# Attention-times-values of the odd mixer: unsplit fp32 products of 64 columns in place of split products of 128

## The chip, the cores and the metric

The kernel runs on one NeuronCore of a Trainium2 chip. The metric is device time in microseconds of one execution; lower is better. The engines are named as the profile names them: PE (TensorE, the matrix array), PEld (its weight loads), DVE (VectorE), ACT (ScalarE), POOL (GpSimd), SP (SyncE, which issues most DMAs).

## The reference, cut to what matters

The program is a two-layer encoder trunk over 512 tokens of width 1024, all in fp32. Each layer runs a half-step FFN, a token mixer, attention into 256 memory tokens, and a second half-step FFN, each followed by a layer norm. The mixer of the odd layer (`mixer_c`) is the part concerned: 16 heads of width 64, where each token attends to a clamped window of 8 rows by 16 columns of the 8 x 64 token grid, with a learned bias.

```
q, k, v = split(h @ w_in, 3)                     # 512 x 1024 each, 16 heads x 64
for each grid row r, column c and head:
    s = q . k_nb * 64**-0.5 + bias               # 8 x 16 = 128 neighbours
    p = softmax(s)
    o = p @ v_nb                                 # the products that change
y = o @ w_out
```

## The kernel before, in words

**Numbers.** Operands of most products are split in two: a part `hi`, which is the value rounded to the reduced format fp32r (ACT writes it: a `CAST`), and the rest `lo` (DVE subtracts). The usual product is then three products of the array: hi·hi, hi·lo, lo·hi (`mm3`). Tokens are ordered by grid column, so that a tile of 128 tokens is 16 grid columns of 8 rows.

**The odd mixer.** Heads go in eight pairs. For each pair `queries` and `keys` project and split; `weights_of` makes the scores in PSUM tiles `a` for four blocks of 128 queries and at most 256 keys, adds the bias, and does the softmax on DVE, ACT and POOL; `turned` transposes the probabilities of both heads on PE into PSUM tiles `t` (two banks a head, 16 transposes a pair) and takes them out into SBUF; `attend` multiplies them with the values into PSUM tiles `d`; the results, split, are the stationary operands of the output projection (`share` for the first four pairs, `down` for the rest). `values(grp, t)` makes the values of four heads for one tile of 128 tokens; there are four groups and four tiles.

In `attend` there are for each head four tiles `j` of 128 keys, and each meets 256 queries. The values are kept split with the two parts side by side: 64 columns of hi and 64 of lo for each head, so one stationary operand has 128 columns. The probabilities are split too, so each (head, j) takes two products of 128 columns by 256, sixteen for a pair. The two halves of a result (partitions 0 to 63 from the hi values, 64 to 127 from the lo values) are then added: ACT copies one half, DVE adds the other, and the sum is split again.

**What sets the order.** The kernel records all its instructions as a graph and a planner (`Graph.plan`) writes out an order for each engine: it keeps a clock for every engine, adds a cost for each instruction (`Graph.cost`), and takes the ready instruction with the smallest key (the place in the program, or in the second pass a latest start worked back from PE's order). Tiles come from rotating pools: 27 SBUF buffers `slab` of 4 KB a partition, 14 buffers `t2` of 2 KB, PSUM banks `a` 3, `d` 2, `t` 3; who needs a buffer waits until an earlier user is done. All instructions are issued from one line, 157 (160 after the change), so groups in the profile are told apart by their tiles: `d<-slab,slab 128x256` in the odd mixer are the products of `attend`, `t<-ident,t` the transposes of `turned`, `t<-xh,slab`, `d<-xh,slab` and the like the projections, `slab<-t` what takes a PSUM bank out (the name `t` stands for a PSUM bank and for the `t2` buffers).

Of the kernel before, what the change touches and what calls it, by code (L numbers as in the profile page):

```python
# [12 lines left out]
F32 = mybir.dt.float32  # L13
F32R = mybir.dt.float32r
# [3 lines left out]
ALU = mybir.AluOpType  # L18
AX = mybir.AxisListType

P = 128
# [44 lines left out]
class Graph:  # L66
# [3 lines left out]

    LATENCY = {"tensor": 200.0, "vector": 115.0, "scalar": 135.0, "gpsimd": 90.0, "sync": 90.0}
    PATIENT = ("vector", "scalar")
    URGENT = ("vector", "scalar", "gpsimd")
    ENGINES = ("tensor", "vector", "scalar", "gpsimd", "sync")

# [36 lines left out]
    @staticmethod  # L112
    def cost(engine, method, out, ins, kw):
        n = 1
        for d in (out if method != "tensor_reduce" else ins[0]).ap[1:]:
            n *= d[1]
        wide = any(z.space == bass.MemoryType.PSUM for z in ins + [out]) if engine != "sync" else False
        if method == "dma_start":
            return 1200.0 if "accum_op" in kw else 600.0
        if engine == "tensor":  # L120
            return max(n / 2.4 + 14, 111)
        scalars = sum(1 for z in ins if z.ap[-1][1] == 1)
        aside = 120.0 * any(Graph.extent(z)[0] > 0 for z in ins + [out])
        if engine == "vector":
            if method == "tensor_scalar" and not wide:
                n = n / 2
            return n / 0.96 + 72 + aside + 60 * scalars + 120 * (method == "scalar_tensor_tensor" and "accum_out" in kw)
        if engine == "scalar":
            scaled = 42 * hasattr(kw.get("scale"), "tensor")
            return n / 1.2 + (55 if wide else 100) + aside + 45 * scalars + 130 * ("accum_out" in kw) + scaled  # L130
        if n <= 8:
            return 270.0 if method == "tensor_scalar" else 200.0 if method != "tensor_tensor" else 390.0 + 157.0 * n
        if method == "memset":
            return n * 0.83 + 60
        dense = len(ins) == 2 and all(z.ap[-1][0] != 0 for z in ins)
        return n * (2.4 if dense else 1.7) + (70 if dense else 130)

    def record(self, engine, method, args, kw):
        kw = dict(kw)
        aps = [z for z in list(args) + list(kw.values()) if hasattr(z, "tensor")]  # L140
        outs = [kw[k] for k in ("out", "accum_out") if k in kw]
        if "out" not in kw:
            outs.insert(0, args[0])
        ins = [z for z in aps if not any(z is o for o in outs)]
        op = Op()
        op.engine, op.index, op.dma, op.adds = engine, len(self.ops), method == "dma_start", "accum_op" in kw
        op.rank = op.index
        op.ns = self.cost(engine, method, outs[0], ins, kw)
        func = args[2] if method == "activation" else None
        op.table = str(func) if func in (AF.Silu, AF.Exp) else None  # L150
        op.size = math.prod(outs[0].shape) * 4
        op.thin = op.dma and engine == "sync" and op.size >= 2**19 and outs[0].shape[0] <= 64
        op.port = method in ("tensor_tensor", "scalar_tensor_tensor", "tensor_scalar") and (
            engine == "gpsimd" or engine == "vector" and math.prod(outs[0].shape[1:]) >= 64 and all(z.space != bass.MemoryType.PSUM for z in ins)
        )
        fn = getattr(getattr(self.nc, engine), method)
        op.call = lambda: fn(*args, **kw)  # L157
        op.deps, op.users, op.frees, op.later = set(), [], [], []
        if self.after and engine in self.after[1]:
            op.deps.add(self.after[0])  # L160
        for z, writes in [(z, False) for z in ins] + [(z, True) for z in outs]:
            info = self.tiles.get(z.tensor.name)
            if info is None:
                continue
            p0, p1, runs = self.extent(z)
            opens = writes and kw.get("start", False)
            keep = []
            for q, w, a0, a1, other in info["log"]:
                over = opens or p0 < a1 and a0 < p1 and (
                    info["bank"] and q.engine != engine or any(l < b and a < h for l, h in runs for a, b in other)  # L170
                )
                if over and (w or writes or info["bank"] and q.engine != engine) and q is not op:
                    op.deps.add(q)
                covered = writes and p0 <= a0 and a1 <= p1 and all(any(l <= a and b <= h for l, h in runs) for a, b in other)
                if not covered:
                    keep.append((q, w, a0, a1, other))
            keep.append((op, writes, p0, p1, runs))
            info["log"] = keep
            info["users"].add(op)
        self.ops.append(op)  # L180

    def plan(self):

# [38 lines left out]
        while len(order) < len(self.ops):  # L222
            best = None
            for e in self.ENGINES:
                arrive(e)
                if ready[e] and e in self.PATIENT:
                    key, _, op = ready[e][0]
# [72 lines left out]
    def emit(self):  # L300
# [10 lines left out]
        for op in self.ops:  # L311
            if op.engine in self.URGENT:
                op.key = last[op]
# [7 lines left out]
class Kernel:  # L321
# [925 lines left out]
    def mixer_c(self, ln_i, last):  # L1247
        nc, a = self.nc, self.a
# [4 lines left out]
        def values(grp, t):  # L1253

            if t == 0:
                wv[0] = self.w_cols_side(w_in, 2 * D + 256 * grp)
                vp[grp] = [self.slab(F32R, (P, 2, 4, 2, 64)) for _ in range(2)]
                if grp == 0:
                    for dst, lo in ((slice(64, 128), 0), (slice(0, 64), 448)):
                        nc.scalar.copy(ends[0][:, :, dst], self.xh[:, :, lo : lo + 64])  # L1260
                        nc.vector.tensor_copy(ends[1][:, :, dst], self.xl[:, :, lo : lo + 64])
            ps = self.ps("t" if grp else "a")
            for k in range(KB):
                x = self.xT(k, 64 + t * P, 64 + (t + 1) * P) if t < 3 else [z[:, k, :] for z in ends]
                self.side_step(ps, x, wv[0][k // 2][:, k % 2], k)
            z, y = vp[grp][t // 2][:, t % 2], self.t2(F32)
            self.side_sum(y[:, :256], ps)
            self.split(y[:, :256].rearrange("p (v c) -> p v c", v=4), z[:, :, 0], z[:, :, 1])

        def queries(pair, first=False):  # L1270

# [81 lines left out]
        def turned(us):  # L1353

            pts = []
            for u in us:
                part = lambda t, j: u[t][:, j * P : (j + 1) * P]
                banks = [
                    [part(0, 1), part(1, 0), part(1, 1), part(2, 0)],
                    [part(2, 1), part(3, 0), part(0, 0), part(3, 1)],  # L1360
                ]
                got = [self.split_t2(self.transposed([(i * P, P, z) for i, z in enumerate(bank)])) for bank in banks]
                pts.append(got)
            return pts

        def attend(pts, pair):
            pos = [self.ps("d") for _ in range(2)]
            for s, po in enumerate(pos):
                for j in range(4):
                    dst = po[:, j * P : j * P + 256] if j < 3 else po.rearrange("p (c n) -> p c n", c=4)[:, 0:4:3]  # L1370
                    v = vp[pair // 2][j // 2][:, j % 2, 2 * (pair % 2) + s].rearrange("p z c -> p (z c)")
                    for i, z in enumerate(pts[s][j // 2]):
                        mv = z[:, (j % 2) * 256 : (j % 2) * 256 + 256]
                        mv = mv.rearrange("p (c n) -> p c n", c=2) if j == 3 else mv
                        nc.tensor.matmul(
                            dst, v, mv, start=j == 0 and i == 0, stop=j == 3 and i == 1, skip_group_check=True
                        )

            o = self.t2(F32)
            for s, po in enumerate(pos):  # L1380
                y = o[64 * s : 64 * s + 64]
                nc.scalar.copy(y, po[64:128])
                nc.vector.tensor_tensor(out=y, in0=po[0:64], in1=y, op=ALU.add)
            return self.split_pair(o)

        def share(n):

# [5 lines left out]
        vp, qs, ks, acts = {}, {}, {}, []  # L1393
        wv, wq, wk, wo = [None], [None], [None], {}
        for t in range(NT):
            values(0, t)
# [4 lines left out]
        for pair in range(8):  # L1401
# [7 lines left out]
            pts = turned(us)  # L1409
# [256 lines left out]
```

## Time and profile before

| | |
|---|---|
| three runs, us | 2127.91, 2128.59 (median), 2130.17 |
| profiled execution: span from the first to the last instruction, us | 2123.9 |
| median of the runs less that span, us | 4.7 |
| PE busy | 2109.2 us, 99% |
| PEld busy | 1871.0 us, 88% |
| DVE busy | 1735.8 us, 82% |
| ACT busy | 1161.2 us, 55% |
| POOL busy | 287.4 us, 14% |

The profile is of one more execution, of which the page gives the span alone; what a run has beside its span (start and end of the program) lies in the 4.7 us. A busy share of PE counts a product from its start to its modelled end, though the next one starts earlier: the step from one start to the next, read from the timeline, is what a product costs in a dense run. The odd mixer's products of `attend` lie between 1434 and 1594 us of the span.

### The profile page before, as it was taken

The page shows a single profiled execution, that of the slowest core. Times are in us where ns is not written, and L with a number is a line of the kernel's source. Part 1 is how long each engine was busy: PE and PEld are TensorE (multiplying, and loading weights), DVE is VectorE, ACT ScalarE, POOL GpSimd, SP SyncE. Part 2 cuts the span into 40 slices and gives each one's busy share as a digit, 9 for nine tenths or more (in the row PEclk, how much of TensorE's full clock was granted, in tenths as well). Part 3 has the DMA queues.
Part 4 walks back from the last instruction along what each step waited for, and adds up shares of the span by engine and source line. Part 5 has one row for each costly group of instructions (what it writes and reads, how often), then busy time and mean ns, then how long its engine had stood idle before and what let it go on. Part 6 is the DMA issues. An engine that isn't in the chain of part 4 may idle for free.

```text
span 2123.9 us, 32745 instructions
## 1 busy us (share of the span) xinstructions
PE 2109.2 (99%) x12648; PEld 1871.0 (88%) x12648; DVE 1735.8 (82%) x2500; ACT 1161.2 (55%) x1903; POOL 287.4 (14%) x379
## 2 busy tenths in 40 slices
PE   9999999999999999999999999999999999999997
PEld 7999988888888899998889999888888888999996
DVE  7789988888748879998879999866577479699997
ACT  5555443698546554545545455457764465444552
POOL 0001015310102000000200000312210021000003
PEclk9999999999999999999999999999999999999999
DMA  6566562004434346564445556356454433456551
GB/s 205 141 168 144 136 191 91 21 18 116 140 125 109 90 117 181 150 158 129 148 100 143 126 139 186 78 147 165 119 165 155 139 93 96 110 149 155 143 149 60
DMA packets 208860, 275.93 MB, mean 130 GB/s; under 512 B 10688, under 2 KB 151616, under 8 KB 208704
## 3 DMA queue, kind: packets, MB, share of 16 engines
q1 hardware_dynamic: 175904, 221.14, 34.0%
q0 software_dynamic: 32512, 52.44, 14.1%
q8 instruction: 100, 1.64, 0.3%
q14 instruction: 56, 0.46, 0.1%
q10 hardware_dynamic: 288, 0.26, 0.0%
HBM read 259.12 MB, written 4.19 MB: 124 GB/s over the span
## 4 chain that ended last, share of the span: by engine, by line
PE 96%; DVE 1%; ACT 1%; DMA 1%; issue 0%; SPq 0%; DVEq 0%; ACTq 0%
PE a L157 59%; PE d L157 23%; PE t L157 15%; DVE slab L157 1%; ACT t L157 1%; DMA slab<-t 1%; DVE x L157 0%; ACT slab L157 0%; SPq L157 0%; DVE t L157 0%; DMA raw<-x_t 0%; ACT xh L157 0%; DVE mn L157 0%; DVE xl L157 0%; DVEq L1662 0%
## 5 line engine op out<-in xcount | busy, mean ns | idle before, releaser
L157 DVE TENSOR_TENSOR slab<-slab,slab 128x1024 fp32r<-128x1024 f32 (+3 forms) x638 | 727.5, 1166 | 69.5 <-ACT slab L157 39.9
L157 ACT CAST slab<-slab 128x1024 fp32r<-128x1024 f32 (+2 forms) x498 | 472.7, 983 | 341.5 <-DVE slab L157 173.2
L157 PE MATMUL a<-slab,slab 128*128 128x256 f32 (+3 forms) x2320 | 567.2, 322 | 0.7 <-DMA slab<-t 0.4
L157 PE MATMUL a<-xh,slab 128*128 128x256 f32 (+2 forms) x2480 | 559.9, 315 | 0.3 <-ACT slab L157 0.3
L157 PE MATMUL d<-slab,slab 128*128 128x512 f32 (+2 forms) x1856 | 447.0, 381 | 0.0
L157 PEld LDWEIGHTS a<-xh,slab 128*128 128x128 f32 x2480 | 416.4, 190 | 33.7 <-ACT slab L157 1.0
L157 PEld LDWEIGHTS a<-slab,slab 128*128 128x128 f32 x2320 | 409.5, 190 | 38.8 <-ACT t L157 1.3
L157 PE MATMUL a<-xl,slab 128*128 128x256 f32 (+1 forms) x1240 | 389.7, 314 | 0.0
L157 PE MATMUL a<-raw,slab 128*128 128x256 f32 x2048 | 388.9, 283 | 0.1
L157 PEld LDWEIGHTS d<-slab,slab 128*128 128x128 f32 x1856 | 329.0, 189 | 55.9 <-issue 0.2
L157 PEld LDWEIGHTS a<-raw,slab 128*128 128x128 f32 x2048 | 327.9, 192 | 5.4 <-ACT slab L157 0.5
L157 PEld LDWEIGHTS a<-xl,slab 128*128 128x128 f32 x1240 | 236.0, 190 | 18.4 <-DVE xl L157 0.4
L157 PE MATMUL t<-slab,slab 128*128 128x512 f32 (+1 forms) x840 | 209.5, 389 | 0.0
L157 DVE TENSOR_TENSOR slab<-raw,slab 128x1024 fp32r<-128x1024 f32 (+2 forms) x140 | 160.2, 1160 | 18.6 <-ACT slab L157 18.4
L157 PEld LDWEIGHTS t<-slab,slab 128*128 128x128 f32 x840 | 149.9, 189 | 26.3
L157 DVE TENSOR_TENSOR slab<-t,slab 128x512 fp32r<-128x512 f32 (+2 forms) x223 | 137.6, 638 | 16.4 <-ACT slab L157 15.9
L157 ACT CAST slab<-t 128x512 fp32r<-128x512 f32 (+2 forms) x223 | 120.9, 566 | 40.7 <-DVE t L157 13.9
L157 ACT CAST slab<-raw 128x1024 fp32r<-128x1024 f32 (+1 forms) x132 | 124.3, 971 | 27.9 <-PE a L157 8.8
L157 DVE SCALAR_TENSOR_TENSOR x<-d,x 128x512 f32<-128x512 f32 x168 | 114.7, 685 | 25.3 <-PE d L157 24.4
L157 ACT COPY t<-a 128x512 f32<-128x512 f32 (+1 forms) x116 | 63.5, 550 | 130.4 <-PE a L157 77.2
L157 POOL DMA_DIRECT2D slab<-ffn_w_down x40 | 47.7, 1193 | 310.3 <-DVE slab L157 276.3
L157 ACT ACTIVATE t<-a 128x512 f32<-128x512 f32 (+3 forms) x65 | 36.3, 559 | 89.0 <-PE a L157 89.0
(126 smaller groups left out, 2167.2 us busy)
## 6 DMA issues: line engine op xcount, KB each, us to landing
slab<-ffn_w_gate SPq DMA_DIRECT2D x80, 512.0 KB
slab<-ffn_w_up SPq DMA_DIRECT2D x80, 512.0 KB
slab<-ffn_w_down SPq DMA_DIRECT2D x80, 512.0 KB
slab<-ffn_w_down POOLq DMA_DIRECT2D x40, 512.0 KB, 5.8
raw<-mem_w_kv SPq DMA_DIRECT2D x16, 1024.0 KB
slab<-t SPq DMA_DIRECT2D x96, 128.0 KB
slab<-ffn_w_gate POOLq DMA_DIRECT2D x16, 512.0 KB, 7.8
slab<-ffn_w_up POOLq DMA_DIRECT2D x16, 512.0 KB, 6.0
```

The costliest lines, as they stand in the source:

```text
L157: op.call = lambda: fn(*args, **kw)
```

## The change

Four things change, all for the odd mixer.

1. `values` no longer splits: the four heads' values of a tile, 256 columns, stay as they are in fp32, in one `slab` a group (before: two, with both parts).
2. `turned` no longer splits the transposed probabilities: each bank is copied once to SBUF as fp32, the first bank of a head by DVE and the second by ACT (before: a `CAST` by ACT and a subtraction by DVE for each bank). One `slab` a head (before: two).
3. `attend` multiplies the unsplit fp32 operands: per (head, j) one product with a stationary operand of 64 columns. The first head of a pair writes partitions 0 to 63 of one PSUM bank, the second partitions 64 to 127, and the products of the two heads alternate. There are eight products a pair and one bank `d` (before sixteen and two). The bank holds both heads' results as they are, and is split straight from PSUM: the copies, additions and the buffer between fall away.
4. The planner: an fp32 product is costed at four passes over its columns, and at half of that where it takes 64 rows or columns; a new method `join` binds the last n instructions into one run (the first waits for what all of them need, each follows the one ahead of it, all but the first have the highest priority), and adds 95 ns to the cost of the first and of the last.

```diff
+    TURN = 95.0
...
         if engine == "tensor":
-            return max(n / 2.4 + 14, 111)
+            passes = 4 if method == "matmul" and ins[0].dtype == F32 else 1
+            beside = 2 if ins[0].shape[0] == 64 or out.shape[0] == 64 else 1
+            return max(n * passes / 2.4 + 14, 111) / beside
...
+    def join(self, n):
+
+        run = self.ops[-n:]
+        for prev, op in zip(run, run[1:]):
+            run[0].deps |= op.deps.difference(run)
+            op.deps.add(prev)
+            op.rank = -1
+        run[0].ns += self.TURN
+        run[-1].ns += self.TURN
...
-                vp[grp] = [self.slab(F32R, (P, 2, 4, 2, 64)) for _ in range(2)]
+                vp[grp] = self.slab(F32, (P, 4, 256))
...
-            z, y = vp[grp][t // 2][:, t % 2], self.t2(F32)
-            self.side_sum(y[:, :256], ps)
-            self.split(y[:, :256].rearrange("p (v c) -> p v c", v=4), z[:, :, 0], z[:, :, 1])
+            self.side_sum(vp[grp][:, t], ps)
...
-                got = [self.split_t2(self.transposed([(i * P, P, z) for i, z in enumerate(bank)])) for bank in banks]
-                pts.append(got)
+                z = self.slab(F32, (P, 2, 512))
+                for i, bank in enumerate(banks):
+                    ps = self.transposed([(i * P, P, y) for i, y in enumerate(bank)])
+                    if i:
+                        nc.scalar.copy(z[:, i], ps)
+                    else:
+                        nc.vector.tensor_copy(z[:, i], ps)
+                pts.append(z)
...
         def attend(pts, pair):
-            pos = [self.ps("d") for _ in range(2)]
-            for s, po in enumerate(pos):
-                for j in range(4):
...
-                    for i, z in enumerate(pts[s][j // 2]):
...
-                        nc.tensor.matmul(
-                            dst, v, mv, start=j == 0 and i == 0, stop=j == 3 and i == 1, skip_group_check=True
-                        )
-
-            o = self.t2(F32)
-            for s, po in enumerate(pos):
-                y = o[64 * s : 64 * s + 64]
-                nc.scalar.copy(y, po[64:128])
-                nc.vector.tensor_tensor(out=y, in0=po[0:64], in1=y, op=ALU.add)
-            return self.split_pair(o)
+            po = self.ps("d")
+            for j in range(4):
+                for s in range(2):
+                    own = po[64 * s : 64 * s + 64]
...
+                    c0 = 64 * (2 * (pair % 2) + s)
...
+                    nc.tensor.matmul(
+                        dst, vp[pair // 2][:, j, c0 : c0 + 64], mv, start=j == 0, stop=j == 3, skip_group_check=True
+                    )
+            nc.join(8)
+            return self.split_t2(po)
```

The order of all engines is the same as before up to the start of the odd mixer, and again from the early part of the memory attention behind it. PE, the first pair's products of `attend`, before (`d_2656` and `d_2657` are the two heads' banks, `a_` tiles are scores of the next pair, `t_2667` values of the next group):

```order
L157 MATMUL a_2641<-slab_2611,slab_2581 128x256 x2
L157 MATMUL d_2656<-slab_2614,slab_2549 128x256 x4
L157 MATMUL d_2656<-slab_2616,slab_2550 128x256 x2
L157 MATMUL d_2656<-slab_2616,slab_2550 128x2x128 x2
L157 MATMUL t_2667<-slab_2661,xh_83 128x512
L157 MATMUL d_2657<-slab_2618,slab_2549 128x256
L157 MATMUL a_2643<-slab_2611,slab_2581 128x192 x2
L157 MATMUL d_2657<-slab_2618,slab_2549 128x256
L157 MATMUL a_2648<-slab_2612,slab_2581 128x192 x2
L157 MATMUL d_2657<-slab_2618,slab_2549 128x256
L157 MATMUL a_2650<-slab_2612,slab_2581 128x256 x2
```

The same place after the change (`slab_2608` and `slab_2611` are the two heads' probabilities, `slab_2549` the group's values):

```order
L160 MATMUL a_2634<-slab_2606,slab_2576 128x256
L160 MATMUL d_2649<-slab_2608,slab_2549 64x256
L160 MATMUL d_2649<-slab_2611,slab_2549 64x256
L160 MATMUL d_2649<-slab_2608,slab_2549 64x256
L160 MATMUL d_2649<-slab_2611,slab_2549 64x256
L160 MATMUL d_2649<-slab_2608,slab_2549 64x256
L160 MATMUL d_2649<-slab_2611,slab_2549 64x256
L160 MATMUL d_2649<-slab_2608,slab_2549 64x2x128
L160 MATMUL d_2649<-slab_2611,slab_2549 64x2x128
L160 MATMUL a_2630<-slab_2606,slab_2576 128x192
```

Before, other products stand between those of the second head; now eight stand together, the heads in turn, between scores of the next pair.

PE, the last pair, whose results the output projection needs, before (`a_3040` and `a_3059` are banks of the output projection):

```order
L157 MATMUL a_3040<-slab_3027,slab_2841 128x512
L157 MATMUL d_3041<-slab_3031,slab_2903 128x256 x4
L157 MATMUL d_3041<-slab_3033,slab_2904 128x256 x2
L157 MATMUL d_3041<-slab_3033,slab_2904 128x2x128 x2
L157 MATMUL d_3042<-slab_3035,slab_2903 128x256 x4
L157 MATMUL d_3042<-slab_3037,slab_2904 128x256 x2
L157 MATMUL d_3042<-slab_3037,slab_2904 128x2x128 x2
L157 MATMUL a_3059<-slab_3048,slab_2897 128x512
```

And after:

```order
L160 MATMUL a_2990<-slab_2979,slab_2812 128x512
L160 MATMUL d_2991<-slab_2982,slab_2868 64x256
L160 MATMUL d_2991<-slab_2985,slab_2868 64x256
L160 MATMUL d_2991<-slab_2982,slab_2868 64x256
L160 MATMUL d_2991<-slab_2985,slab_2868 64x256
L160 MATMUL d_2991<-slab_2982,slab_2868 64x256
L160 MATMUL d_2991<-slab_2985,slab_2868 64x256
L160 MATMUL d_2991<-slab_2982,slab_2868 64x2x128
L160 MATMUL d_2991<-slab_2985,slab_2868 64x2x128
L160 MATMUL d_3006<-slab_2996,slab_2862 128x512
```

Sixteen products in two banks became eight in one; what stands around them is the output projection in both.

ACT, the second pair, where it takes the transposed banks out, before (`t_2681` to `t_2687` are PSUM banks):

```order
L157 CAST slab_2682<-t_2681 128x512
L157 CAST slab_2684<-t_2683 128x512
L157 CAST slab_2686<-t_2685 128x512
L157 CAST slab_2688<-t_2687 128x512
L157 ACTIVATE t_2609_2690<-d_2689 128x512
```

And after (`t_2671`, `t_2674`; `t_2664` is a projection's bank, `raw_2720` a loaded weight):

```order
L160 CAST t_2584_2665<-t_2664 128x512
L160 CAST slab_2723<-raw_2720 128x1024
L160 COPY slab_2669<-t_2671 128x512
L160 COPY slab_2672<-t_2674 128x512
L160 ACTIVATE t_2595_2676<-d_2675 128x512
```

ACT now takes two of the four banks and DVE the other two; before, both engines worked on each. Over the program ACT's order has 48 rows fewer than before, and DVE's also 48.

More of the change, by code (lines that the diff above doesn't have):

```diff
@@ L1361, in turned @@
                 ]
-                got = [self.split_t2(self.transposed([(i * P, P, z) for i, z in enumerate(bank)])) for bank in banks]
-                pts.append(got)
+                z = self.slab(F32, (P, 2, 512))
[6 more added lines that the diff above has]
+                pts.append(z)
             return pts
         def attend(pts, pair):
-            pos = [self.ps("d") for _ in range(2)]
-            for s, po in enumerate(pos):
-                for j in range(4):
-                    dst = po[:, j * P : j * P + 256] if j < 3 else po.rearrange("p (c n) -> p c n", c=4)[:, 0:4:3]
-                    v = vp[pair // 2][j // 2][:, j % 2, 2 * (pair % 2) + s].rearrange("p z c -> p (z c)")
-                    for i, z in enumerate(pts[s][j // 2]):
-                        mv = z[:, (j % 2) * 256 : (j % 2) * 256 + 256]
-                        mv = mv.rearrange("p (c n) -> p c n", c=2) if j == 3 else mv
-                        nc.tensor.matmul(
-                            dst, v, mv, start=j == 0 and i == 0, stop=j == 3 and i == 1, skip_group_check=True
-                        )
-            o = self.t2(F32)
-            for s, po in enumerate(pos):
-                y = o[64 * s : 64 * s + 64]
-                nc.scalar.copy(y, po[64:128])
-                nc.vector.tensor_tensor(out=y, in0=po[0:64], in1=y, op=ALU.add)
-            return self.split_pair(o)
+            po = self.ps("d")
+            for j in range(4):
+                for s in range(2):
+                    own = po[64 * s : 64 * s + 64]
+                    dst = own[:, j * P : j * P + 256] if j < 3 else own.rearrange("p (c n) -> p c n", c=4)[:, 0:4:3]
+                    c0 = 64 * (2 * (pair % 2) + s)
+                    mv = pts[s][:, j // 2, (j % 2) * 256 : (j % 2) * 256 + 256]
+                    mv = mv.rearrange("p (c n) -> p c n", c=2) if j == 3 else mv
+                    nc.tensor.matmul(
[3 more added lines that the diff above has]
+            return self.split_t2(po)
         def share(n):
```

## The prediction

> **What bounds the kernel now.** I read the page first, then who PE waited for, then the timeline of PE at the places that change.
>
> ```profile
> span 2123.9 us, 32745 instructions
> ...
> PE 2109.2 (99%) x12648; PEld 1871.0 (88%) x12648; DVE 1735.8 (82%) x2500; ACT 1161.2 (55%) x1903; POOL 287.4 (14%) x379
> ...
> PEclk9999999999999999999999999999999999999999
> ...
> PE 96%; DVE 1%; ACT 1%; DMA 1%; issue 0%; SPq 0%; DVEq 0%; ACTq 0%
> ```
>
> PE is busy throughout, at the full granted clock in every slice, and the chain that ended last is PE for 96%. A high share alone could still hide waits, so next comes what PE waited for between 1320 and 1620 us, which holds the odd mixer, and how busy the others are in two stretches of it:
>
> ```profile
> PE t L157 <- DVE x L157: 0.7, 1, 0.7
> PE a L157 <- DMA slab<-t: 0.4, 2, 0.2
> PE a L157 <- DVE slab L157: 0.4, 1, 0.4
> ```
>
> ```profile
> core 0: us, PE busy (x) PEld busy (x) DVE busy (x) ACT busy (x) POOL busy (x), PEclk, DMA share, GB/s
> 1480.00:1520.00 40.00, 40.00 (x231) 34.64 (x231) 23.55 (x65) 30.47 (x80) 9.56 (x22) 1.00 0.53 140
> ...
> 1560.00:1600.00 40.00, 39.82 (x214) 33.78 (x213) 30.89 (x59) 24.78 (x51) 1.10 (x2) 1.00 0.53 172
> ```
>
> PE waited 1.5 us in all in these 300 us. DVE works 23.55 and 30.89 of 40 us, ACT 30.47 and 24.78. So the stage is bound by the steps of PE, and work taken off DVE and ACT can return at most what PE waits for them. The question is what the new products cost PE.
>
> **What the old products cost.** The last pair's products stand undisturbed in PE's timeline (start, duration, count):
>
> ```profile
> 1589.83 1.52 PE L157 MATMUL a<-slab,slab 128*128 128x512 f32 x6
> 1591.19 2.08 PE L157 MATMUL d<-slab,slab 128*128 128x256 f32 x16
> 1593.10 1.09 PE L157 MATMUL a<-slab,slab 128*128 128x512 f32 x4
> 1594.03 1.30 PE L157 MATMUL d<-slab,slab 128*128 128x512 f32 x5
> ...
> L157 PE MATMUL d<-slab,slab x159: 276/283/397, 1379.7 to 1599.9; 128*128 128x256 f32 x128, 128*128 128x512 f32 x31
> ```
>
> From 1591.19 to 1593.10 are 1.91 us for 16 products, 0.119 us each, and the last row gives their count in the mixer: 128, so eight pairs cost 8 x 1.91 = 15.3 us. Behind them four products of 512 columns take 0.93 us, 0.23 each: 256 columns more cost 0.11, so nearly the whole step is the streaming of columns. One product's record lasts 0.283 us though the next starts after 0.119: 0.16 us is the array's run-out, which a dense run hides.
>
> **What the new products cost.** Eight a pair, 64 in all, each 256 columns of unsplit fp32 against 64 stationary columns. No row of this trace shows such a product, so its cost is bounded. The nearest row in kind is the old pair of products: it spells out the full product of two split operands, four part products (hi and lo of the values times hi and lo of the probabilities) of 64 columns each. If the array has to form the same four parts itself, an unsplit product is four passes of 256 columns: 4 x 0.119 = 0.48 us for one alone, and half of that, 0.24, if the other head's product runs in the other 64 columns at the same time. A run of eight is then 8 x 0.24 = 1.91 us, exactly the old time: sixteen steps of a full array became sixteen steps of two halves. From below, by pure streaming (0.11), 16 x 0.11 = 1.76 us, 0.15 less. From above, if the halves never overlap, 8 x 0.48 = 3.82 us. The weight loads change nothing in this: the 1.91 us held 16 loads of 128 columns, and four loads of 64 columns for each of eight products are the same 2048 columns. I take full overlap at four passes, since both heads have their own half of the array and of the bank, the order alternates them with nothing between, and no row shows a half array being refused; that is where the doubt lies, and both ends stay in the range.
>
> [...]
>
> **The turn.** Each run changes the kind of product going in and coming out. The nearest row for that is PE's change to fp32 transposes and back:
>
> ```profile
> 1448.17 0.39 PE L157 MATMUL t<-xl,slab 128*128 128x512 f32 x1
> 1448.39 0.39 PE L157 MATMUL t<-xh,slab 128*128 128x512 f32 x1
> 1448.63 1.03 PE L157 MATMUL t<-ident,t 128*128 128x128 f32 x8
> 1449.42 0.48 PE L157 MATMUL d<-xh,slab 128*128 128x512 f32 x1
> 1449.73 0.40 PE L157 MATMUL d<-xl,slab 128*128 128x512 f32 x1
> 1449.96 0.40 PE L157 MATMUL d<-xh,slab 128*128 128x512 f32 x1
> ```
>
> Going in, the step is 0.24 where 0.22 stands ahead of it; coming out it is 0.31 where 0.23 follows: 0.10 us for both. If instead the array runs empty at each end, it is the run-out twice, 0.33 us; and if the halves run half a product out of step, the last half stands alone for 0.24 more. Between 0.10 and 0.57 a run I take 0.20, nearer to the measured row: 8 x 0.20 = +1.6 us; both ends are +0.8 and +4.6.
>
> [...]
>
> **What else falls away.** The rows for it, in the mixer's stretch from 1380 to 1600 us:
>
> ```profile
> L157 DVE TENSOR_TENSOR slab<-t,slab 128x512 fp32r<-128x512 f32 x40 | 26.4, 686 | 3.6 <-ACT slab L157 3.3
> L157 ACT CAST slab<-t 128x512 fp32r<-128x512 f32 x40 | 22.8, 597 | 4.7 <-PE t L157 3.5 <-DVE t L157 0.8
> ...
> L157 DVE TENSOR_TENSOR t<-d,t 64x512 f32<-64x512 f32 x16 | 10.9, 682 | 3.5 <-ACT t L157 3.4
> L157 ACT COPY t<-d 64x512 f32<-64x512 f32 x16 | 9.3, 583 | 1.7 <-PE d L157 1.4
> ...
> L157 DVE TENSOR_TENSOR slab<-t,slab 128x256 fp32r<-128x256 f32 x16 | 6.3, 421 | 3.6 <-ACT slab L157 3.5
> L157 ACT CAST slab<-t 128x256 fp32r<-128x256 f32 x16 | 6.2, 403 | 1.5 <-DVE t L157 1.5
> ```
>
> The x40 are 32 splits of transposed banks and 8 of results. The 32 become 16 copies on each engine (taken at the price of the casts and subtractions), the 8 stay but read PSUM, and the x16 all go. ACT saves 16 x 0.597 + 16 x 0.583 + 16 x 0.403 = 25.3 us, DVE 16 x 0.686 + 16 x 0.682 + 16 x 0.421 = 28.6 us. All of it lies beside PE's work, which covers it now: it is worth what PE's waits are worth. Of the 1.5 us, 0.7 belongs to the layer norm ahead of the mixer. Waits shorter than the run-out do not count as idle; a place where one can be seen:
>
> ```profile
> 1546.82 0.47 PE L157 MATMUL a<-slab,slab 128*128 128x192 f32 x2
> 1547.13 0.30 PE L157 MATMUL d<-slab,slab 128*128 128x256 f32 x1
> 1547.52 0.33 PE L157 MATMUL a<-slab,slab 128*128 128x192 f32 x1
> ```
>
> One product steps 0.39 in place of 0.12, 0.27 lost. I put the relief at 0.6 us, between nothing and 2.0. The freed buffers (two `slab` a pair, one a group, one bank `d` a pair) let weights load earlier, which nothing on PE waits for.
>
> The bound run adds a wait: its first product waits for the probabilities of both heads, where before the first head's eight could go ahead. Behind it on PE stand the next pair's scores, for which DVE and ACT wait with the softmax. The order puts scores and projections ahead of the run to cover the copies of the last bank, one copy of about 0.6 us in place of a cast and a subtraction; without that cover a pair would lose up to that 0.6 us, 4.8 in all. I cost it at nothing, since the copy is the shorter path.
>
> **The sum.** Products 0, turn +1.6, relief -0.6: span 2123.9 + 1.0 = 2124.9 us. The median of the runs lies 4.7 us above the profiled span (2128.6 against 2123.9), so 2129.6 us. The forecast's own range: -1.2 (streaming price) - 2.0 (relief) + 0.8 (turn) to +4.6, which is 2126.2 to 2133.2.
>
> **The rivals.** About 0.2%, 4.3 us, is what a measurement of this kernel tells from no change. Slower begins where a run of eight costs over 0.53 us more, 2.44 us, that is where a product steps by more than 0.30 us; full overlap is 0.24, none 0.48.
>
> *One after the other.* The two halves take turns, because PE finishes one product before it begins the next. For it: no row shows two products at once; PE's records overlap by the run-out alone. Against it: nothing of a half is shared, by the order. Price: 8 x (3.82 - 1.91) = +15.3 us at 0.119, +13.0 at 0.11; with the turn some 2143 us (2141 to 2146).
>
> *Overlap at the seam only.* If a product is issued as its four passes, in order, the other head's first pass can only join the last of them: three of four passes stand alone. A run is 8 x 3 x 0.119 + 0.119 = 2.98 us, +8.5 us in all (+6.6 by streaming), 2135 to 2139. For it: PE's starts are in order in every row above. Against: if a product is issued in two pieces of two passes, the same reasoning gives 2 x 0.119 x 8 + 0.24 = 2.14, which is the forecast with its out-of-step end.
>
> *Fewer passes.* The transposes are fp32 too, and eight of them take 0.79 us, 0.10 for 128 columns, one pass and no more. If unsplit products took two passes, the runs would cost half, -7.6 us: 2122 us; one pass, 2118. Against it: a transpose only moves values, and a full product needs the four parts above.
>
> *The change does not do what it says*: products could be torn apart by the planner. The rows of the order show the eight together at the first and the last pair, so I give it nothing.
>
> **How the numbers follow.** Forecast 0.65, one after the other 0.14, seam only 0.11, fewer passes 0.06, and 0.04 for a larger turn or relief than bounded, split evenly between slower and the rest. So slower by over 0.2%: 0.14 + 0.11 + 0.02 = 0.27; faster: 0.06 + 0.01 = 0.07; within: 0.66. The time is the forecast's, 2129.6. The range runs from 2125, below the forecast's own, to 2138, which takes in the seam; it leaves out one-after-the-other and fewer passes, 0.20.
>
> **What would show it.** In the changed profile, PE's timeline at the last pair: eight rows of `d<-slab,slab` with 64 columns, from the first start to the next product's start 1.9 to 2.3 us confirms the sum; about 3.0 the seam, 3.8 no overlap, 1.0 fewer passes. The step ahead of and behind the run gives the turn. DVE and ACT should lose 25 to 30 us each in the mixer with PE's end unmoved: if the end follows them, my reading of what bounds the stage is wrong. PE's waits between 1320 and 1620 us should stay under 2 us; more would show the bound run waiting for its copies.

## The result: slower, by waits that the products did not cause

The changed kernel takes 2138.3 us (median of four runs, 2135.4 to 2140.2) against 2128.6 before: a ratio of 1.0047, 95% interval 1.0033 to 1.0061. That is +9.7 us, above the range of 2125 to 2138, and on the side to which 0.27 was given.

The page of the changed kernel, its lines on the span and the engines:

```profile
span 2137.0 us, 32614 instructions
...
PE 2113.9 (99%) x12648; PEld 1866.8 (87%) x12648; DVE 1710.7 (80%) x2452; ACT 1137.4 (53%) x1855; POOL 289.9 (14%) x379
```

The span grew by 13.1 us in the profiled execution. DVE lost 25.1 us of work and ACT 23.8, a little less than the prediction had (28.6 and 25.3). PE is busy 4.7 us longer, though its number of records is the same.

The first pair's products in PE's timeline (start, duration, records):

```profile
1437.14 0.51 PE L160 MATMUL a<-slab,slab 128*128 128x192 f32 x3
1437.58 1.95 PE L160 MATMUL d<-slab,slab 128*64 128x256 f32 x16
1439.46 0.62 PE L160 MATMUL a<-slab,slab 128*128 128x192 f32 x3
```

From 1437.58 to 1439.46 the run of eight takes 1.88 us, turn included; before, the undisturbed sixteen took 1.91. Each product of 64 columns shows as two records. So the two halves overlap, and the products themselves became no dearer. The cost lies elsewhere. Who PE waited for between 1320 and 1640 us:

```profile
PE a L160 <- DMA slab<-t: 7.4, 5, 3.7
PE t L160 <- DVE x L160: 0.7, 1, 0.7
PE a L160 <- DVE slab L160: 0.4, 1, 0.4
```

The first row was 0.4 us before. `slab<-t` are the small moves, 128 KB each, that `queries` and `keys` make through SP's queue to set the split parts of each head into both halves of the partitions; the scores `a` need them. The longest wait is at the last pair (an idle time and its releaser stand in brackets):

```profile
1573.17 1.95 PE L160 MATMUL d<-slab,slab 128*64 128x256 f32 x16
1578.81 0.50 PE L160 MATMUL a<-slab,slab 128*128 128x192 f32 x1 [3.68 <-DMA slab<-t]
1579.66 4.43 PE L160 MATMUL a<-slab,slab 128*128 128x192 f32 x15 [0.35 <-DMA slab<-t]
...
1584.16 8.13 PE L160 MATMUL a<-slab,slab 128*128 128x512 f32 x27
```

After it PE is slow: the granted clock (the column behind POOL's) in the 10.3 us from 1577.3 is 0.52, and 1.00 ahead and behind.

```profile
1577.30:1587.60 10.30, 8.36 (x26) 6.91 (x27) 3.97 (x19) 6.65 (x24) 0.00 (x0) 0.52 0.47 148
1570.00:1577.00 7.00, 5.12 (x31) 3.41 (x29) 2.52 (x3) 0.61 (x2) 0.00 (x0) 1.00 1.01 310
1588.00:1598.00 10.00, 10.00 (x53) 8.32 (x52) 6.67 (x8) 4.88 (x6) 0.00 (x0) 1.00 0.31 101
```

PE is busy for 8.36 us of these, at about half speed: some 4 us lost. With 7.0 us more of waits that is 11 of the 13.1 us.

Why the moves were late is read from SP's queue and from the landings. First the changed kernel, then the one before, at the last pair (start, time from the first issue to the end of the last, count):

```profile
1558.14 1.11 SPq L160 DMA_DIRECT2D slab<-t  x2
1564.79 1.62 SPq L160 DMA_DIRECT2D raw<-c_w_out  x2
1566.66 11.47 SPq L160 DMA_DIRECT2D slab<-t  x8
1578.28 0.48 SPq L160 DMA_DIRECT2D raw<-c_w_out  x1
```

```profile
1556.41 0.37 SPq L157 DMA_DIRECT2D raw<-c_w_out  x1
1562.09 5.07 SPq L157 DMA_DIRECT2D slab<-t  x8
1567.25 7.43 SPq L157 DMA_DIRECT2D raw<-c_w_out  x3
```

Two loads of the output projection's weights (512 KB and 1 MB) went ahead of the eight moves, and the eight took 11.47 us to issue in place of 5.07. The program's order of SP, with the semaphores that each DMA waits for, shows why the issue took so long:

```
L160 DMA raw_2978<-c_w_out 128x2x512 [waits DMAHW4_49,DMAHW0_49,DVE_49]
L160 DMA raw_2995<-c_w_out 128x2x1024 [waits DMAHW5_49,DMAHW1_49,DVE_49]
L160 DMA slab_2924<-t_2841_2922 64x512 [waits DMAHW6_49,Activation_49]
L160 DMA slab_2924<-t_2841_2922 64x512 [waits DMAHW7_49]
L160 DMA slab_2924<-t_2842_2923 64x512 [waits DVE_49]
L160 DMA slab_2924<-t_2842_2923 64x512
L160 DMA slab_2925<-t_2841_2922 64x512 [waits DMAHW2_49,PE_49]
L160 DMA slab_2925<-t_2841_2922 64x512 [waits DMAHW3_49]
L160 DMA slab_2925<-t_2842_2923 64x512 [waits DMAHW4_49]
L160 DMA slab_2925<-t_2842_2923 64x512 [waits DMAHW5_49]
```

The DMAs of SP use eight semaphores in turn. The last move waits for `DMAHW5_49`, which the 1 MB load took eight places ahead: it is not issued until that load has landed, and SP waited 6.3 us for it.

```profile
SPq L160 <- DMA raw<-c_w_out: 6.3, 1, 6.3
```

But that was not PE's wait. The other seven moves were out by 1571.33, and the chain of work that ended last runs through one of these (start, time from issue to landing); below it is the move on the chain of the kernel before:

```profile
1568.61 10.91 DMA slab<-t
...
1566.55 4.07 DMA slab<-t
```

By the semaphore events in the trace, the 1 MB load, issued at 1566.04, lands at 1577.65, and the moves land behind it in the order of their issue. The first two, issued at 1566.66 and 1567.18, land at 1578.21 and 1578.67 and end the wait of 3.68 us: 11.6 us from issue to landing for the first, where the first move took 4.9 us before the change. The eighth lands at 1580.75, and PE has no idle time before the score that needs it, at 1582.04. So in this trace the moves that PE waited for were late in their transfer behind the load, and not in their issue.

SP's loads were not alone in that stretch. POOL sent two weights of the layer norm, 512 KB each, at the same time (before the change one left at 1561.69 and the other, behind the moves, at 1570.65). From 1568 to 1576 they took 37.1% of the DMA engines' time (queue q0, 1.04 MB) beside 51.8% for SP's queue (q1):

```profile
1566.08 0.56 POOL L160 DMA_DIRECT2D slab<-ln_g  x1 [9.77 <-PE t L160]
1566.64 0.54 POOL L160 DMA_DIRECT2D slab<-ln_b  x1
...
q1 hardware_dynamic: 425, 1.28, 51.8%
q0 software_dynamic: 283, 1.04, 37.1%
```

At the second pair SP's load delays the moves by itself. There a 1 MB load goes out at 1413.38, the first of eight moves behind it at 1415.35, and this move lands after 8.6 us; the move at the same place before the change, issued at 1414.10 with no load just ahead, landed after 2.2 us. PE waits 2.19 us, and from 1413.4 to 1424 SP's queue has the DMA engines to itself:

```profile
1424.62 0.59 PE L160 MATMUL a<-slab,slab 128*128 128x192 f32 x3 [2.19 <-DMA slab<-t]
...
q1 hardware_dynamic: 2385, 2.91, 104.1%
```

### The profile page after: what moved, and what is told of

It is laid out like the page before. It is cut to its first block, busy times and chain, and to the rows that moved or that the text cites. A ratio compares the mean times of both kernels' runs of the same rounds, so it can differ in the third digit from the quotient of the medians.

```text
span 2137.0 us, 32614 instructions
## 1 busy us (share of the span) xinstructions
PE 2113.9 (99%) x12648; PEld 1866.8 (87%) x12648; DVE 1710.7 (80%) x2452; ACT 1137.4 (53%) x1855; POOL 289.9 (14%) x379
## 4 chain that ended last, share of the span: by engine, by line
PE 95%; DMA 3%; DVE 1%; ACT 1%; issue 0%; SPq 0%; DVEq 0%; POOL 0%; POOLq 0%; ACTq 0%
PE a L160 57%; PE d L160 23%; PE t L160 15%; DMA slab<-t 1%; DMA raw<-c_w_in 1%; DVE slab L160 0%; ACT slab L160 0%; DVE x L160 0%; DMA slab<-ffn_w_up 0%; ACT t L160 0%; DVE t L160 0%; DMA raw<-x_t 0%; SPq L160 0%; ACT xh L160 0%; DVE mn L160 0%
## 5 line engine op out<-in xcount | busy, mean ns | idle before, releaser
L160 PE MATMUL d<-slab,slab 128*128 128x512 f32 (+3 forms) x1856 | 441.0, 388 | 0.0
L160 PEld LDWEIGHTS d<-slab,slab 128*128 128x128 f32 (+1 forms) x1856 | 319.2, 185 | 61.4 <-issue 1.6
L160 DVE TENSOR_TENSOR slab<-raw,slab 128x1024 fp32r<-128x1024 f32 (+2 forms) x140 | 159.9, 1158 | 25.8 <-ACT slab L160 25.1
L160 DVE TENSOR_TENSOR slab<-t,slab 128x512 fp32r<-128x512 f32 (+3 forms) x179 | 109.9, 630 | 22.1 <-ACT slab L160 21.5
L160 ACT CAST slab<-t 128x512 fp32r<-128x512 f32 (+2 forms) x167 | 92.3, 574 | 36.2 <-DVE t L160 13.4
```

## The experiments

**Theory L (loads)**: the change needs fewer buffers `slab`; weights that wait for buffers are split earlier, the two raw buffers come free earlier, and the planner lets the next weight load go ahead of the small moves. The moves land late, PE waits, its clock drops. **Rival S (scores)**: the order on PE is at fault, since lighter DVE and ACT let the planner bring scores forward, whatever SP does. **Rival B (bound run)**: the run of eight took away the products that covered the moves. The kernel before took 2126.9 us on each of the two chips that made the runs below; times are to be held against that. The change itself was not run on these two; against it, ratios to the kernel before are compared (1.0047 for the change).

**The old amount of buffers.** The instructions of the change, but the values in two slabs a group and the probabilities in two a head, each half used:

```diff
-                vp[grp] = self.slab(F32, (P, 4, 256))
+                vp[grp] = [self.slab(F32, (P, 4, 256)) for _ in range(2)]
...
-            self.side_sum(vp[grp][:, t], ps)
+            self.side_sum(vp[grp][t // 2][:, t % 2], ps)
...
-                z = self.slab(F32, (P, 2, 512))
+                z = []
                 for i, bank in enumerate(banks):
...
+                    z.append(self.slab(F32, (P, 2, 512)))
                     if i:
-                        nc.scalar.copy(z[:, i], ps)
+                        nc.scalar.copy(z[i][:, 0], ps)
...
```

> The change with the old amount of buffers: two slabs for each group's values and two for each head's transposed probabilities, each half used; all instructions as in the change. Theory L (loads: the freed buffers let the weight loads for the mixer go ahead of the small moves of queries and keys in SP's queue, the moves land late, PE waits for them and its clock drops): the loads fall back behind the moves, PE's waits for moves fall from 7.4 us to under 1.5, the granted clock is 0.998 as before the change, and the time is 2127.5 to 2130. Rival S (scores: DVE and ACT have less to do, so the order brings the next pair's scores forward, ahead of their moves, whatever SP does) and rival B (the bound run of eight takes away the cover ahead of the scores): both stay as they are here, so 2135 to 2140 with 5 us or more of waits for moves.

Measured: 2126.7 us, ratio 1.0002 (0.9993 to 1.0011). L's times were reckoned from the other chip's 2128.6; with the 1.7 us between the chips taken off, it forecast 2125.8 to 2128.3. The waits for moves:

```profile
PE a L160 <- DMA slab<-t: 0.6, 2, 0.4
```

The waits are gone with the new products, the light DVE and ACT and the bound run all in place. S and B both forecast 5 us or more here and fall, as far as they blame these alone. At the last pair SP sends a load of 512 KB ahead of the moves and the 1 MB behind them, and POOL's two loads leave behind them too (1570.76 and 1571.88; the moves from 1562.46).

**The old order of SP's DMAs.** The change with its freed buffers, where a hold in the planner makes SP issue the mixer's DMAs in the sequence of before (the hold adds no wait to the program; `SP_ORDER`, left out here, lists that sequence by places in the program):

```diff
         for op in self.ops:
-            op.wait, op.ready = len(op.deps) + len(op.frees), 0.0
+            op.wait, op.ready = len(op.deps) + len(op.frees) + op.held, 0.0
...
+            for u in op.then:
+                release(u, stop)
...
+PINNED = list(zip(SP_ORDER, SP_ORDER[1:]))
...
+        loads = [op for op in self.ops if op.engine == "sync"]
+        for x, y in PINNED:
+            loads[x].then.append(loads[y])
+            loads[y].held += 1
```

> The change as it is, with the freed buffers, but SP issues its DMAs of the odd mixer in the order that they had before the change (an order alone, no wait is added to the program). Theory L: the waits go and the time is 2127.5 to 2130, as with the old buffers. Rival S or B: waits of 5 us or more stay, 2135 to 2140. A third reading, that the early loads themselves take the DMA engines from the moves only where both fall together: 2128 to 2132, with part of the waits.

Measured: 2125.2 us, ratio 0.9994 (0.9984 to 1.0003), a granted clock of 0.998.

```profile
PE a L164 <- DMA slab<-t: 0.7, 1, 0.7
```

With the buffers free and SP's order put back, the loss is gone: the buffers act through the order of the DMAs. The hold alone is the edit, but it shifts POOL's two loads as well: they leave at 1555.58 and 1556.14, some 6 us ahead of the first of the last pair's moves (1562.01), in place of 0.6 and 0.02 us ahead of it. How much of the delay at the last pair came from SP's loads ahead in the queue and how much from POOL's beside it, no run separates. The third reading's time (2128 to 2132) is missed, but with both kinds of load out of the moves' way the run says nothing against it. The median lies 0.6 us below even L's adjusted range.

**The last two loads alone** behind the last pair's moves, by the same hold on two pairs of DMAs; the earlier loads stay as the change has them:

```diff
+PINNED = [(397, 402), (397, 403)]
```

> The change, but only the last two loads of the output projection's weights are put behind the last pair's eight moves; the earlier loads stay ahead of their moves. Theory L: the wait at the last pair goes (4.1 us at one step, 1.5 in those that follow) and with it the half-clock stretch (10.2 us at half speed, 5.1 lost), the waits of the second and fourth pair stay (2.6 and 1.7 us): 2129.5 to 2132. If the half clock comes from something else than that wait, 2134 to 2137. Rival S or B: 2135 to 2140.

Measured: 2127.6 us, ratio 1.0004 (0.9994 to 1.0013). That is a little under L's forecast, even when 1.7 us are taken off it (2127.8 to 2130.3).

```profile
PE a L163 <- DMA slab<-t: 2.9, 2, 2.3
...
1423.42 0.59 PE L163 MATMUL a<-slab,slab 128*128 128x192 f32 x3 [2.31 <-DMA slab<-t]
```

The wait at the second pair stays, 2.31 us, and the clock does not drop (0.998 over the execution). With these two loads behind the moves the loss can no longer be measured, though the early loads stay ahead of theirs. POOL's loads, too, leave earlier here, 1558.99 and 1559.55, against 1565.0 for the first move.

**The complement**: the early loads behind their moves, the last two ahead as in the change.

```diff
+PINNED = [(313, 342), (318, 347), (333, 349), (341, 370), (346, 375), (361, 377), (369, 398), (374, 399), (347, 348), (375, 376)]
```

> The complement of the run with only the last loads moved: the early loads stand behind their moves as before the change, the last two loads of the output projection's weights stay ahead of the last pair's eight moves. Theory L: the waits of the second and fourth pair go, the wait at the last pair stays (3.5 to 4.5 us at one step) and brings the half-clock stretch of 10.2 us with it: 2132 to 2136, granted clock 0.996. If the half clock needs several waits in a row, not one, the clock stays at 0.998 and the time is 2128 to 2131.

Measured: 2133.1 us, ratio 1.0028 (1.0019 to 1.0037), a granted clock of 0.997. PE's timeline and the clock of the stretch behind the wait:

```profile
1568.09 1.95 PE L163 MATMUL d<-slab,slab 128*64 128x256 f32 x16
1572.24 0.33 PE L163 MATMUL a<-slab,slab 128*128 128x192 f32 x1 [2.21 <-DMA slab<-t]
1573.03 1.43 PE L163 MATMUL a<-slab,slab 128*128 128x192 f32 x6 [0.46 <-DMA slab<-t]
```

```profile
1570.00:1573.00 3.00, 0.36 (x3) 0.19 (x2) 0.00 (x0) 0.58 (x1) 0.00 (x0) 1.00 0.99 255
1572.50:1579.50 7.00, 6.45 (x23) 5.36 (x23) 3.87 (x19) 5.35 (x20) 0.00 (x0) 0.56 0.55 186
```

As L forecast, though with a smaller wait (2.2 us at the step in place of 3.5 to 4.5). Two loads in the wrong place, with POOL's beside them (1561.01 and 1561.57, the first move at 1561.91), cost 6 to 8 us against the kernel before and the run with SP's old order: 2.7 us of waits, some 3 us of half clock behind them (6.45 us busy at 0.56), and a rest that was not placed.

**Unbound.** The call that joins the eight products is left out.

```diff
-            nc.join(8)
```

> The change without the binding of the eight products into one run (the method that joins them is not called, so the planner may put other products between). Theory L: the loads stand ahead of the moves here too, so the waits stay: 2134 to 2141. Rival B: the waits for moves go, under 1.5 us in all, and the time is 2128 to 2131, or up to 2133 if each break of a run costs a turn of 0.15 us.

Measured: 2144.4 us, ratio 1.0083 (1.0068 to 1.0098), the slowest of all and above L's 2134 to 2141, which counted nothing for a broken run. The wait for moves is there, 5.1 us, so B falls from the other side too: binding is no cause, it helps. Its timeline shows why, and gives the price of one product by itself, which the prediction could only bound:

```profile
PE a L160 <- DMA slab<-t: 5.1, 3, 4.1
...
1461.34 0.65 PE L160 MATMUL d<-slab,slab 128*64 128x256 f32 x2
1461.91 0.47 PE L160 MATMUL a<-slab,slab 128*128 128x192 f32 x2
1462.31 0.65 PE L160 MATMUL d<-slab,slab 128*64 128x256 f32 x4
1462.90 0.50 PE L160 MATMUL t<-slab,xh 128*128 128x512 f32 x1
```

Two records, one product, take 0.57 us to the next start; four records, two products of different heads, take 0.59. A second head is free, and a product torn from its neighbour costs as much as two. With eight in 1.88 us, each further couple costs about (1.88 - 0.59) / 3 = 0.43 us and the turn about 0.16 us.

**Heads in blocks**, with the old order of SP: the first head's four products, then the second's.

```diff
-            for j in range(4):
-                for s in range(2):
+            for s in range(2):
+                for j in range(4):
```

> The change with the old order of SP's DMAs, and in each run of eight products the first head's four stand ahead of the second head's four (before: in turn). If two products overlap because neighbours in the order use different halves of the array, a run takes 7 x 0.43 + 0.15 = 3.2 us (only the fourth and fifth overlap) in place of 1.88, +10 us: 2134 to 2138. If the array works on both halves whatever the order, a run stays at 1.9 us and the time at 2125 to 2128.

Measured in a single run: 2133.2 us, no wait for moves. The first pair's run:

```profile
1434.33 0.88 PE L164 MATMUL a<-slab,slab 128*128 128x192 f32 x6
1435.13 2.86 PE L164 MATMUL d<-slab,slab 128*64 128x256 f32 x16
1437.93 0.96 PE L164 MATMUL a<-slab,slab 128*128 128x192 f32 x6
```

A run takes 2.80 us (1435.13 to 1437.93), between the 3.2 of the seam and the 1.88 of heads in turn: 8 x 0.92 = 7.4 us, which answers the 8.0 us between this run and the median with the old order of SP. Neither forecast is met: order matters, but the overlap reaches further than the two neighbours at the change of heads.

**A margin for the moves**, an attempt at a version that beats both: the old order of SP, and the planner counts each move as landing 1 us later.

```diff
-                lands = finish + 790.0
+                lands = finish + 790.0 + 1000.0 * (kind and op.size == 2**17)
```

> The change with the old order of SP's DMAs, and the planner counts each small move of queries and keys as landing 1 us later, so that it places the scores later on PE. If the rest of the waits for moves (0.7 us with the old order of SP) and the lost steps around them can be covered, PE's waits for moves are 0 and the time is 2123.5 to 2125.5, 0.9985 to 0.9995 of the kernel before. If the planner pays for the later scores with waits elsewhere, 2125.5 to 2129.

Measured: 2125.9 us (11 runs, 2124.9 to 2131.3) against 2126.9, ratio 0.9998 (0.9989 to 1.0007), in the range for a planner that pays elsewhere and not in that for a gain. PE waits for no move any more; its remaining waits are those that it had before the change:

```profile
PE t L164 <- DVE x L164: 0.7, 1, 0.7
PE a L164 <- DVE slab L164: 0.4, 1, 0.4
```

It beats the change by its ratio, and cannot be told from the kernel before: with the waits for moves gone, the medians are 1 us apart, and by the interval the new products are worth 2.3 us at most.

## Why the prediction was wrong

**What bounds the kernel** held: PE. 25 us less work on DVE and 24 on ACT moved nothing by themselves.

**The products** were right. The sum had four passes and full overlap of the halves: 1.91 us a run, and with the turn 2.11. Measured were 1.88 in all: about 0.43 for each couple of products, four steps of 0.11, which is the price by pure streaming that stood as the lower bound, and 0.16 for the turn, inside the 0.10 to 0.57. That a product is four passes was the author's estimate, from the four part products that the old pair spelled out, and no run shows the passes: each product appears as two records on PE and two weight loads of 64 columns on PEld (sixteen of each in the first pair's run of eight, where the prediction reckoned thirty-two loads), and 0.43 us a couple is what was measured. The 0.33 us reckoned for an array that runs empty at both ends of a run is twice the 0.16.

**The rivals on the product** fell: one after the other (3.8 us a run) and fewer passes (1.0) by the first pair's 1.88. The seam is how PE behaves in part when the heads are not in turn (2.80 in place of 1.88); with the order of the change it does not arise. That 2138.3 lies in the seam's 2135 to 2139 is chance.

**The step that failed** is one sentence: "The freed buffers (two `slab` a pair, one a group, one bank `d` a pair) let weights load earlier, which nothing on PE waits for." Nothing waits for the weights; but they travel in the queue of the small moves for which PE's scores do wait. The earlier loads stood ahead of the moves, the moves behind them took 11.6 us to land in place of 4.9, and this was not priced: 7.0 us of waits. The first two runs show it from both ends: the old buffers with the new products, and the new buffers with the old order of SP, each within the error of the kernel before, and the complement shows that the two last loads ahead of the moves cost 0.28%, with POOL's loads in the same place as in the change. What followed was not on the list either: the clock fell to half at the last pair's wait (4.0 us in two parts) and cost some 4 us more, so that the price of that wait was about doubled. The prediction's sign of being wrong did show, waits of 8.5 us where it allowed 2, but it would have read them as the bound run waiting for its copies.

**The relief** of 0.6 us is within the noise of what is left: with the moves covered, the medians differ by 1 us and the ratio's interval holds 1.

**The bound run** was costed at nothing, and without it the kernel is slower. The prediction did not give the reason: the run does not only avoid turns, it keeps each product beside its partner (0.57 us for a product by itself, 0.59 for two of different heads).

What stays open: some 2 us of the 13.1 in the profiled execution were not placed. And at the last pair no run keeps POOL's loads away from the moves while SP's loads stand ahead of them, so the share of each in the longest wait, and whether the clock would have dropped without POOL's, is not known.

## What to carry to other kernels

A change that frees buffers can move loads forward, as it did here; look in the order of the queue for what these loads now stand ahead of, above all small transfers on the bound engine's path, and for what other queues send at the same time. Then ask of a late transfer whether its issue or its landing was late, and which one the engine waited for: here the longest delay of an issue (6.3 us, by the eight semaphores) was not the one that PE felt. Two 64-column fp32 products in the two halves of the array cost here what one costs (0.59 and 0.57 us), where they alternate and stay together; with the heads in blocks a run of eight took 2.80 us in place of 1.88.

## What the runs showed of the hardware that was not expected

The granted clock fell to half after a wait shorter than the half-speed stretch that came with it: 2.21 and 0.46 us of idle time (PE busy 0.36 of 3.00 us) went with 7 us at 0.56. A wait of 2.31 us at the second pair, in the run with only the last loads moved, left the clock at 0.998. So the size of a single wait does not decide it in these runs. The clock's records in the trace of the change begin and end on a grid of 3.4133 us: half speed lasts 10.24 us there, three steps of it, the full speed ahead of it, 1573.54 us, is 461, and the full speed behind it, 542.72 us, is 159. In the complement (a granted clock of 0.997 over the execution) half speed lasts 6.83 us, two steps. Here are the steps that end with the drop, in the change and in the complement, and the emptier of the two on which the 2.31 us fall (PE's busy time stands behind the length):

```profile
1574.25:1577.66 3.41, 0.87 (x10) 0.29 (x4) 0.00 (x0) 0.59 (x1) 0.00 (x0) 1.00 1.02 260
1569.94:1573.35 3.41, 0.74 (x6) 0.54 (x5) 0.00 (x0) 0.58 (x1) 0.00 (x0) 1.00 1.04 258
1419.53:1422.94 3.41, 1.58 (x7) 0.96 (x6) 0.67 (x1) 2.17 (x2) 0.00 (x0) 1.00 0.98 217
```

The clock dropped behind 0.87 and 0.74 us of work in a step and not behind 1.58; three steps do not give a threshold, and what decides the drop is not shown by these runs.

An fp32 product of 64 columns by 256 appears as two records; with the other head's product beside it, the two take about 0.43 us in a run of eight, and with the heads in blocks, where a product's partner stands four places behind it, some overlap is left (2.80 us a run, against some 3.2 reckoned for an overlap of the two neighbours at the change of heads alone).
